# Two transformer blocks on one core: sums of squares in four TensorE strips, splits without GpSimd, the overflow branch in the last expert group

## The chip, the core and the metric

The kernel runs on one core of one Trainium2 chip. The metric is the device time of one execution in microseconds (us); the time of a kernel is the median of its runs. Names: PE is TensorE, DVE is VectorE, ACT is ScalarE, POOL is GpSimd, SP is the queue that issues the loads.

## What is computed

256 tokens of width 1024 go through two blocks. The first has a hybrid mixer (a state-space scan and a gated short convolution, each with a grouped RMS norm) and a mixture of 32 experts; the second has another mixer and a dense feed-forward layer. The change concerns two parts of the first block:

```python
ssd_out = grouped_rmsnorm(y * jax.nn.silu(z), ssd_norm, SSD_GROUPS)   # 2 groups of 512 channels
sc = sc_b * causal_depthwise_conv(sc_c * sc_v, sc_conv_w)
sc_out = grouped_rmsnorm(sc, sc_norm, SC_GROUPS)                      # 16 groups of 64 channels
return jnp.concatenate([ssd_out, sc_out], axis=-1) @ w_out
...
# experts: two of 32 for each token
return (jax.nn.silu(xb @ w_gate[e]) * (xb @ w_up[e])) @ w_down[e]
```

Each expert has a table of a fixed number of tokens. If one gets more, a branch computes the surplus; with these inputs it is not taken.

## The kernel before

**Precision.** Products of the mixer are fp32-exact in three passes: a weight tile of 128x1024 is split into a high and a low half (`hilo`, L316 to 330), the high by ScalarE, the low by `lo_on[0]`, which is VectorE (L330), or GpSimd for the units whose numbers stand in `POOL_A` (42, 43, 45, 47). TensorE then runs high x high, low x high and high x low (L339 to 341 for columns, L309 to 311 for rows).

**The first mixer.** 45 column units (each 128 columns of the input projection: 8 steps of the contraction, 3 products each) and 16 row units of the output projection are run by `run_units`, which splits a unit's weights two units ahead of its products. A table written by hand (`at`, `later`) sets which small steps stand between the units. The last eight column units, 37 to 44, are the gates z: `after_z(j)` multiplies by the row scale (VectorE), takes silu (ScalarE), and multiplies into `xs` (`gate`, L790: GpSimd for j below 6, VectorE for 6 and 7). Units 45 to 60 are the output projection, the short-convolution half first.

**Sums of squares.** For each of the eight 128-channel tiles of the short convolution (`do_scsq`, L875 to 884) and of the scan (`do_ysq`, L770 to 780) ScalarE squares the tile, and one unit later TensorE adds it over the channels with a constant of ones as stationary operand: 16 columns of `half` into rows 0 to 15 of the PSUM tile `sums`, or 2 columns of `col4` into rows 32 and 33. Sixteen fp32 products in all. After the eighth, `rows_rstd` copies the rows out (ScalarE), turns them to tokens by two transposes (L648), computes the reciprocal root on VectorE (L809 and `rsqrt_of`, L242 to 247: a step for the epsilon, two that seed, three rounds of three), and turns them back (L654). `do_sc_scale` and `do_ssd_scale` then scale the tiles, `split_rows` splits them, and the output projection uses them. `route` copies the transposed hidden state, by ScalarE or VectorE, for the router.

**The experts.** Eight groups of four experts: products `g`, then `u`, then down. The four experts of a group run in four strips of 32 rows of the array (`products`, L1184 to 1189; down, L1212). The weights stream through a ring of raw tiles; SP issues each load in program order, when the tile is free, and `products` and `down` issue the loads of a later group behind their own products. The last down tiles are loaded in smaller pieces (`last_loads`).

**The branch.** `overflow()` reads the largest table size on every engine (`values_load`, L1254) and opens a `tc.If`. It stands in the group g = 3 behind the products `u`, before down. At its start and end SP waits until the loads that are out have landed.

Of the kernel before, what the change touches and what calls it, by code (L numbers as in the profile page):

```python
# [8 lines left out]
F32 = mybir.dt.float32  # L9
# [4 lines left out]
ALU = mybir.AluOpType  # L14
# [20 lines left out]
LEAD = 5  # L35
WARM2 = 4
LOP = ()
NRP = ()
SCS = (42, 42, 44, 45)
SPL = (43, 46)  # L40
FS = 2
POOL_A = (42, 43, 45, 47)
W0 = 5
ORDER = (("xs", 2048, 1), ("sc", 2048, 1), ("scc", 1024, 1), ("hnh", 2048, 1), ("hnl", 2048, 1), ("rsb", 256, 1),
         ("bc", 1024, 1), ("wdt", 128, 1), ("dtx", 256, 1), ("ac", 256, 1), ("ach", 256, 1), ("cb", 768, 1),
# [24 lines left out]
def kernel(ctx: ExitStack, tc: tile.TileContext, *aps, dbg=None, stage=9):  # L70
# [120 lines left out]
    alog = const.tile([128, 16], F32, name="alog")  # L191
    nc.gpsimd.dma_start(alog, bass.AP(tensor=A["a_log"].tensor, offset=A["a_log"].offset, ap=[[0, 128], [1, 16]]))

    half = const.tile([128, 30], F32, name="half")
    V.memset(half, 0.0)
    V.memset(half[0:64, 14:15], 1.0)
    V.memset(half[64:128, 15:16], 1.0)
    col4 = const.tile([128, 7], F32, name="col4")
    V.memset(col4, 0.0)
    V.memset(col4[:, 3:4], 1.0)  # L200
    wfirst = const.tile([128, NE], F32, name="wfirst")
# [1 line left out]
    slots = const.tile([128, 128], F32, name="slots")  # L203
    G.iota(slots, pattern=[[1, 128]], base=-FAR, channel_multiplier=0, allow_small_or_imprecise_dtypes=True)
    sel = const.tile([64, 16], F32R, name="sel")
    fold = const.tile([64, 32], F32, name="fold")
    cols1 = const.tile([128, 128], F32, name="cols1")
    cols2 = const.tile([128, 128], F32, name="cols2")
    dskip = const.tile([128, 8], F32, name="dskip")
# [9 lines left out]
    def late_sel():  # L219
        V.memset(sel.bitcast(F32), 0.0)  # L220
        for r in (0, 32):
            V.tensor_copy(sel[r:r + 16, :], ident[:16, :16])
        V.tensor_tensor(fold, ident[0:64, 0:32], ident[0:64, 32:64], op=ALU.add)

    def late_loads():
        ds_ap = A["d_skip"]
# [123 lines left out]
    def later(n, f, *args):  # L350
        at(cur[0] + n, f, *args)
# [14 lines left out]
    def run_units(units, ahead=2, ready=(), pool=lambda i: False):  # L366


        n = len(units)
        ready = list(ready)  # L370
        while len(ready) < min(ahead, n):
            ready.append(units[len(ready)][0]())
        prev = None
        for i in range(n):
            cur[0] = i
            lo_on[0] = G if pool(i + ahead) else V
            for f, args in pre.pop(i, []):
                f(*args)
            if len(ready) <= i + ahead < n:
                ready.append(units[i + ahead][0]())  # L380
            res = units[i][1](ready[i])
            ready[i] = None
            if prev:
                prev()
            for f, args in due.pop(i, []):
                f(*args)
            prev = (lambda f=units[i][2], r=res: f(r)) if units[i][2] else None
        lo_on[0] = V
        cur[0] = n
        if prev:  # L390
            prev()
        while due or pre:
            cur[0] = min([*due, *pre])
            for f, args in pre.pop(cur[0], []) + due.pop(cur[0], []):
                f(*args)
# [183 lines left out]
        across(y, dg)  # L579

    ps = psum_a.enter_context(tc.tile_pool(name="psA", bufs=1, space=PSUM, reuse_waits="tile"))
    sums = ps.tile([64, T], F32, name="sums")

    def scale_rows():
        p = ps.tile([128, T], F32, name="tp", tag="tp")
# [57 lines left out]
    def turned(dst_shape, rows):  # L643

        n = rows.shape[0]
        pt = ps.tile(dst_shape, F32, name="tp", tag="tp")
        for b in range(2):
            P.transpose(pt[:, b, :n], rows[:, b * 128:(b + 1) * 128], ident[:n, :n])  # L648
        return pt
# [117 lines left out]
            P.matmul(p[i * 64:(i + 1) * 64, 128:256], xdt["t"][:, 1, c], e[:, i, 256:384], start=False, stop=True)  # L767
        V.scalar_tensor_tensor(xs[:, j, :], xs[:, j, :], dskip[:, j:j + 1], p, op0=ALU.mult, op1=ALU.add)

    def do_ysq(j):  # L770
        sq = work.tile([128, T], F32, name="sq", tag="sq", bufs=2)
        S.activation(sq, xs[:, j, :], AF.Square)
        g = j // 4

        def sm():
            P.matmul(sums[32:34, :], col4[:, 3 - g:5 - g], sq, start=(j == 0), stop=(j == 7))
            if j == 7:
                rows_rstd(sums[32:34, :], 2, 512, "ssd")

        later(1, sm)  # L780


    def after_z(j):
        def f(o):
            z = work.tile([128, T], F32, name="cacc", tag="cacc", bufs=2)
            V.tensor_tensor(z, o, rsb, op=ALU.mult)
            S.activation(z, z, AF.Silu)

            def gate():
                (G if j < 6 else V).tensor_tensor(xs[:, j, :], xs[:, j, :], z, op=ALU.mult)  # L790
                later(1, do_ysq, j)

            later(j < 7, gate)
            if j % 4 == 3:
                load_next()

        return f
# [2 lines left out]

    def rows_rstd(src, n, c, key):

        v = work.tile([16, T], F32, name="rr", tag="rr")
        sst[key] = hl = work.tile([64, T], F32R, name="hl", tag="hl")
        V.memset(hl.bitcast(F32), 0.0)
        S.activation(v[:n], src, AF.Copy, scale=1.0 / c)

        def mid():
            V.tensor_scalar(ts32[0][:, :, :n], turned([128, 2, 16], v[:n])[:, :, :n], EPS, None, op0=ALU.add)  # L809
            x, y, t = [i[:, :, :n] for i in ts32]  # L810
            (rsqrt_pool if key in NRP else rsqrt_of)(x, y, t)

        def end():
            stacked(hl, turned_back(ts32[1], n)[:n], n)

        later(1, mid)
        later(2, end)
# [55 lines left out]
        return f  # L873

    def do_scsq(j):  # L875
        sq = work.tile([128, T], F32, name="sq", tag="sq", bufs=2)
        S.activation(sq, sc[:, j, :], AF.Square)

        def sm():
            P.matmul(sums[0:16, :], half[:, 14 - 2 * j:30 - 2 * j], sq, start=(j == 0), stop=(j == 7))  # L880
            if j == 7:
                rows_rstd(sums[0:16, :], 16, 64, "sc")

        later(1, sm)

    def src(nm):
        return lambda: R[nm]
# [63 lines left out]
    def route(a, n=None):  # L951

        if not ROUTED:
            ROUTED["h"] = work.tile([128, 8, T], F32, name="hT", tag="xdt")
        hT = ROUTED["h"]
        if n is None:
            L = ROUTED[a] = ps.tile([128, 36], F32, name="L", tag="acb", bufs=2)
            for k in range(8):
                P.matmul(L, hT[:, k, a * 128:(a + 1) * 128], wr[:, k, :], start=(k == 0), stop=(k == 7))
            return  # L960
        pt = ps.tile([128, 4, 128], F32, name="tp", tag=("mm", "tp", "mm", "yp")[2 * a + n], bufs=(3, 1, 3, 1)[2 * a + n])
        for kk in range(4):
            P.transpose(pt[:, kk, :], h[:, a, n * 512 + kk * 128:n * 512 + (kk + 1) * 128], ident)
        d = hT[:, 4 * n:4 * n + 4, a * 128:(a + 1) * 128]
        if n:
            V.tensor_copy(d, pt)
        else:
            S.activation(d, pt, AF.Copy)
# [16 lines left out]
    korder = list(range(8, 16)) + list(range(8))  # L985
    units += [row_unit(k, i) for i, k in enumerate(korder)]
    at(48, lambda: S.activation(small.tile([128, 1], F32, name="one"), ones[:, 0:1], AF.Sqrt))
    run_units(units, ready=early, pool=lambda i: i in POOL_A)

    ss = small.tile([128, 2], F32, name="ss")  # L990
    L = [ROUTED[a] for a in range(2)]
# [136 lines left out]
    with ExitStack() as pp:  # L1128
# [51 lines left out]
        def products(g, m):  # L1180

            p = P1[m] = ps.tile([128, 512], F32, name="p1", tag="p1", bufs=2)
            for k in range(8):
                for i in range(4):  # L1184
                    r = slice(32 * i, 32 * i + 32)
                    P.matmul(p[r], XS[g][:, k, r], ew(4 * g + i, m, k), start=(k == 0), stop=(k == 7))  # L1186
            for i in range(4):
                if (4 * g + i, m) not in odd:
                    load_expert()
# [15 lines left out]
        def down(g, fs):  # L1205
            if g not in PY:
                PY[g] = [ps.tile([128, 512], F32, name=f"py{n}") for n in range(2)]
            for f in fs:
                for n in range(2):
                    for i in range(4):  # L1210
                        r = slice(32 * i, 32 * i + 32)
                        P.matmul(PY[g][n][r], HT4[g][:, f, r], ew(4 * g + i, "d", f)[:, n * 512:(n + 1) * 512],  # L1212
                                 start=(f == 0), stop=(f == 3))
            if 3 in fs:
                for i in range(4):
                    if (4 * g + i, "d") not in odd:
                        load_expert()

        ysb = {}

# [173 lines left out]
        for g in range(NG):  # L1394
            end = g == NG - 1
            products(g, "g")
            gate_silu()
            if g == 0:
                gates()
                slots_of(1)  # L1400
            else:
                for a, n, _ in HALF:
                    combine(g - 1, a, n)
            slots_back(g)
            slots_turn(g)
            if end:
                for i in range(4):
                    h_turned(i)
            products(g, "u")
            turn(g)  # L1410
            if not end:
                gather(g + 1, 0)
                gather(g + 1, 1)
            if g < NG - 2:
                slots_of(g + 2)
            if g == 1:
                block2_consts()
            if g == 3:
                overflow()
            if end:  # L1420
                mr_stack.close()
                pools2()
                down(g, range(3))
                keep_warm(ps, WARM3, "p2")
                down(g, [3])
                split2(1)
            else:
                down(g, range(4))
            y_out(g)
# [612 lines left out]
```

## Time and profile before

| | |
|---|---|
| median of three runs | 1019.81 us (1016.51 to 1022.83) |
| profiled execution, its own time | 1019.49 us |
| its span | 1017.7 us |
| TensorE busy | 878.6 us (86%) |
| VectorE busy | 433.2 us (43%) |
| ScalarE busy | 318.9 us (31%) |
| GpSimd busy | 146.6 us (14%) |
| read from HBM | 285.87 MB, 282 GB/s over the span |

The span is cut into three stages: the first mixer, the experts, the second block. The shares are means over stages that have different limits, so a share is read within one stage. The durations in the rows below come from this one execution.

### The profile page before, as it was taken

Reading aid. Unit: us, or ns where it says so; the run is one execution under the profiler, and the core shown is the slowest. Engines: PE = TensorE matmul, PEld = TensorE weight load, DVE = VectorE, ACT = ScalarE, POOL = GpSimd, SP = SyncE. Lnnn points to the kernel's source line nnn. Section 1 sums busy time; section 2 is a strip of 40 time slices with the busy share of each in tenths; the row PEclk is TensorE's granted clock in tenths of the full one; section 3 lists DMA queues with packets and bytes.
Section 4 is the critical chain, followed back from the end, with each engine's and each line's share of the span. In section 5 each row is a group of like instructions: output and inputs, shape, how many; then the busy total and the mean of one; then the engine's idle time right before and its main releaser. Section 6 shows DMA issues by size and latency. Waiting matters only on the chain.

```text
span 1017.7 us, 13571 instructions
## 1 busy us (share of the span) xinstructions
PE 878.6 (86%) x5631; PEld 622.3 (61%) x5632; DVE 433.2 (43%) x756; ACT 318.9 (31%) x533; POOL 146.6 (14%) x126
## 2 busy tenths in 40 slices
PE   9989998999978677696667869689689999999997
PEld 8988887678424224241322415137568789999996
DVE  6897575564110111101001110017896776555554
ACT  5565454534001101000000100006355555444444
POOL 4323024002000000000000000003432232111112
PEclk9999999999998789787778988799889999999999
DMA  9496324268999999998999999999625345575301
GB/s 295 114 389 222 138 112 153 95 225 336 425 428 429 427 426 430 426 425 352 427 428 427 428 428 428 428 410 379 232 83 207 96 153 166 169 245 170 120 1 42
DMA packets 77824, 287.85 MB, mean 283 GB/s; under 512 B 12547, under 2 KB 41406, under 8 KB 66238
## 3 DMA queue, kind: packets, MB, share of 16 engines
q1 hardware_dynamic: 77062, 285.55, 71.6%
q8 instruction: 46, 0.75, 0.3%
q0 software_dynamic: 448, 1.08, 0.3%
q10 hardware_dynamic: 248, 0.30, 0.1%
q14 instruction: 20, 0.16, 0.0%
HBM read 285.87 MB, written 1.05 MB: 282 GB/s over the span
## 4 chain that ended last, share of the span: by engine, by line
PE 33%; DMA 13%; DVE 5%; ACT 1%; issue 1%; POOL 0%; SPq 0%; DVEq 0%; ACTq 0%; POOLq 0%
DMA raw<-in_w_up_dram 11%; PE mm L339 5%; PE mm L341 5%; PE mm L340 5%; PE po L309 3%; PE po L311 3%; PE po L310 3%; PE p L1186 3%; PE py L1212 3%; PE gp L1169 2%; DMA rawx<-in_w_down_dram 2%; DVE xf L1528 1%; DVE wab L1493 0%; PE op L1676 0%; PE op L1678 0%
## 5 line engine op out<-in xcount | busy, mean ns | idle before, releaser
L1186 PE MATMUL p<-raw,xse 128*32 128x512 f32 x1008 | 182.5, 722 | 82.6 <-DMA raw<-in_w_gate_dram 48.3
L339 PE MATMUL mm<-hnh,hi 128*128 128x256 f32 x808 | 232.7, 288 | 2.0 <-ACT cx L702 1.3
L341 PE MATMUL mm<-hnh,lo 128*128 128x256 f32 x808 | 227.9, 282 | 1.5 <-DVE lo L330 1.4
L340 PE MATMUL mm<-hnl,hi 128*128 128x256 f32 x808 | 227.3, 281 | 0.0
L330 DVE TENSOR_TENSOR lo<-raw,hi 128x1024 fp32r<-128x1024 f32 x137 | 168.9, 1237 | 80.5 <-ACT hi L329 80.5
L329 ACT ACTIVATE hi<-raw 128x1024 fp32r<-128x1024 f32 x152 | 159.1, 1057 | 100.7 <-PE mm L340 39.8
L1186 PEld LDWEIGHTS p<-raw,xse 128*32 128x32 f32 x1008 | 40.3, 129 | 214.7 <-issue 94.0
L339 PEld LDWEIGHTS mm<-hnh,hi 128*128 128x128 f32 x808 | 152.8, 189 | 11.4 <-issue 7.5
L341 PEld LDWEIGHTS mm<-hnh,lo 128*128 128x128 f32 x808 | 152.8, 189 | 2.5 <-DVE lo L330 2.3
L340 PEld LDWEIGHTS mm<-hnl,hi 128*128 128x128 f32 x808 | 153.2, 190 | 0.9
L1249 DVE TENSOR_TENSOR h<-h,pc 128x512 f32<-128x512 f32 x32 | 20.5, 684 | 140.2 <-PE pc L1247 140.2
L1374 POOL TENSOR_TENSOR g<-h,gain 128x512 f32<-128x512 f32 x2 | 3.5, 1786 | 461.8 <-DVE h L1249 461.8
L1169 PE MATMUL gp<-oh,xnf 128*128 128x128 f32 x256 | 64.6, 412 | 5.1 <-ACT xse L1176 5.1
L1169 PEld LDWEIGHTS gp<-oh,xnf 128*128 128x128 f32 x256 | 62.1, 334 | 6.4 <-ACT xse L1176 6.4
L1212 PE MATMUL py<-raw,hs 128*32 128x512 f32 x480 | 64.5, 635 | 1.2 <-ACT hs L1203 0.7
L1198 DVE TENSOR_TENSOR sg<-sg,p 128x512 f32<-128x512 f32 x8 | 5.5, 688 | 113.4 <-PE p L1186 113.4
L1193 ACT ACTIVATE sg<-p 128x512 f32<-128x512 f32 x8 | 4.8, 599 | 148.3 <-PE p L1186 138.0
L1927 POOL TENSOR_TENSOR sgf<-sgf,rsb 128x256 f32<-128x256 f32 x22 | 31.7, 1441 | 134.4 <-ACT sgf L1926 134.4
L1203 ACT ACTIVATE hs<-p 128x512 f32<-128x512 f32 x8 | 4.8, 597 | 135.7 <-PE p L1201 135.7
L330 POOL TENSOR_TENSOR lo<-raw,hi 128x1024 fp32r<-128x1024 f32 x15 | 37.3, 2499 | 39.7 <-ACT hi L329 39.7
L1212 PEld LDWEIGHTS py<-raw,hs 128*32 128x32 f32 x480 | 19.9, 116 | 32.4 <-issue 27.7
L1174 DVE COPY xse<-gp 128x512 f32<-128x512 f32 x8 | 5.5, 692 | 74.8 <-PE gp L1169 74.8
(469 smaller groups left out, 1160.6 us busy)
## 6 DMA issues: line engine op xcount, KB each, us to landing
raw<-in_w_gate_dram SPq DMA_DIRECT2D x32, 2048.0 KB
raw<-in_w_up_dram SPq DMA_DIRECT2D x31, 2048.0 KB
raw<-in_w_down_dram SPq DMA_DIRECT2D x27, 2048.0 KB
raw<-in_w_in_dram SPq DMA_DIRECT2D x14, 2048.0 KB
raw<-in_w_ffn_in_dram SPq DMA_DIRECT2D x22, 1024.0 KB
raw<-in_w_out_dram SPq DMA_DIRECT2D x6, 2048.0 KB
raw<-in_w_ffn_out_dram SPq DMA_DIRECT2D x5, 2048.0 KB
raw<-in_w_down_dram SPq DMA_DIRECT2D x12, 512.0 KB
```

The costliest lines, as they stand in the source:

```text
L309: P.matmul(po[a, j], yh[:, ts], wh[:, 0, ns], start=(i == 0), stop=False)
L310: P.matmul(po[a, j], yh[:, ts], wl[:, 0, ns], start=False, stop=False)
L311: P.matmul(po[a, j], yl[:, ts], wh[:, 0, ns], start=False, stop=end)
L329: S.activation(hv[:, r], src[:, r], AF.Copy)
L330: lo_on[0].tensor_tensor(lv, src, hv.bitcast(F32), op=ALU.subtract)
L339: P.matmul(o, wh, xh, start=first, stop=False)
L340: P.matmul(o, wh, xl, start=False, stop=False)
L341: P.matmul(o, wl, xh, start=False, stop=last)
L1169: P.matmul(p[:, kk, :], xn[:, a, 4 * hf + kk::8], OT[g][:, a, :], start=(a == 0), stop=(a == 1))
L1186: P.matmul(p[r], XS[g][:, k, r], ew(4 * g + i, m, k), start=(k == 0), stop=(k == 7))
L1212: P.matmul(PY[g][n][r], HT4[g][:, f, r], ew(4 * g + i, "d", f)[:, n * 512:(n + 1) * 512], start=(f == 0), stop=(f == 3))
L1927: G.tensor_tensor(t, t, rsb, op=ALU.mult)
```

## The change

1. **Sums.** `do_scsq` and `do_ysq` call a new `quarter_sums`. Squares are kept until there are four; one unit after the fourth, four products of 32 columns each write four strips of 32 rows of a `sums` tile [128, 2, 256]. The second four add to the same strips. `rows_rstd` copies 128 rows, and two products with a constant `fold` add the four strips and turn them to tokens, in place of the two transposes. `half`, `col4` and `fold` get wider. The squares lie in four buffers, two of them taken from `dtx` and `ac`.
2. **GpSimd.** `POOL_A` goes, so the low halves of units 42, 43, 45 and 47 are made by VectorE; the gate products of j below 6 move to VectorE too. An option for a reciprocal root on GpSimd, unused before, is removed.
3. **Router copy.** One of four copies of the transposed state (second half of the columns, second half of the tokens) moves from VectorE to ScalarE.
4. **Branch.** `overflow()` moves from group 3 to the last group, behind its products `g`, the combine step and the slots, ahead of `h_turned` and of the products `u`. The loads that `products(7, "g")` issued are now issued behind the branch (`next_loads`).

```diff
-POOL_A = (42, 43, 45, 47)
...
-        V.tensor_tensor(fold, ident[0:64, 0:32], ident[0:64, 32:64], op=ALU.add)
+        V.tensor_tensor(fold, ident[:, 0:16], ident[:, 32:48], op=ALU.add)
+        for i in (64, 96):
+            V.tensor_tensor(fold, fold, ident[:, i:i + 16], op=ALU.add)
...
-    sums = ps.tile([64, T], F32, name="sums")
+    sums = ps.tile([128, 2, T], F32, name="sums")
...
+    def quarter_sums(m, j, x, sel_, key, n, c):
+        q = j % 4
+        if q == 0:
+            sqs[m] = []
+        four = sqs[m]
+        sq = work.tile([128, T], F32, name="sq", tag=("sq", "sq", "dtx", "ac")[q], bufs=2 if q < 2 else 1)
+        S.activation(sq, x, AF.Square)
+        four.append(sq)
+        def sm():
+            for i in range(4):
+                P.matmul(sums[32 * i:32 * i + 32, m, :], sel_(j - 3 + i), four[i], start=(j == 3), stop=(j == 7))
+            if j == 7:
+                rows_rstd(sums[:, m, :], n, c, key)
+        if q == 3:
+            later(1, sm)
...
     def do_ysq(j):
-        sq = work.tile([128, T], F32, name="sq", tag="sq", bufs=2)
-        S.activation(sq, xs[:, j, :], AF.Square)
-        g = j // 4
-        def sm():
-            P.matmul(sums[32:34, :], col4[:, 3 - g:5 - g], sq, start=(j == 0), stop=(j == 7))
-            if j == 7:
-                rows_rstd(sums[32:34, :], 2, 512, "ssd")
-        later(1, sm)
+        quarter_sums(1, j, xs[:, j, :], lambda j: col4[:, 3 - j // 4:35 - j // 4], "ssd", 2, 512)
...
-                (G if j < 6 else V).tensor_tensor(xs[:, j, :], xs[:, j, :], z, op=ALU.mult)
+                V.tensor_tensor(xs[:, j, :], xs[:, j, :], z, op=ALU.mult)
...
-        v = work.tile([16, T], F32, name="rr", tag="rr")
+        v = work.tile([128, T], F32, name="rr", tag="rr")
-        S.activation(v[:n], src, AF.Copy, scale=1.0 / c)
+        S.activation(v, src, AF.Copy, scale=1.0 / c)
         def mid():
-            V.tensor_scalar(ts32[0][:, :, :n], turned([128, 2, 16], v[:n])[:, :, :n], EPS, None, op0=ALU.add)
+            pt = ps.tile([128, 2, 16], F32, name="tp", tag="tp")
+            for b in range(2):
+                P.matmul(pt[:, b, :n], v[:, b * 128:(b + 1) * 128], fold[:, :n], start=True, stop=True)
+            V.tensor_scalar(ts32[0][:, :, :n], pt[:, :, :n], EPS, None, op0=ALU.add)
...
-        if n:
+        if n > a:
             V.tensor_copy(d, pt)
...
-    run_units(units, ready=early, pool=lambda i: i in POOL_A)
+    run_units(units, ready=early)
...
+            if (g, m) != (NG - 1, "g"):
+                next_loads(g, m)
+        def next_loads(g, m):
             for i in range(4):
                 if (4 * g + i, m) not in odd:
                     load_expert()
...
             if end:
+                overflow()
+                next_loads(g, "g")
                 for i in range(4):
                     h_turned(i)
             products(g, "u")
...
-            if g == 3:
-                overflow()
```

TensorE, between the last column unit and the first row unit, before (`sums` is the sum of squares, `po` the output projection, `scb` the row scale of the short convolution):

```order
L341 MATMUL mm<-hnh,lo 128x256
L835 MATMUL scb<-hl,selb 128x256 x2
L776 MATMUL sums<-sq,col_131 2x256
L309 MATMUL po<-hi,yhi 128x512
L310 MATMUL po<-lo,yhi 128x512
L311 MATMUL po<-hi,ylo 128x512
```

and of the change:

```order
L341 MATMUL mm<-hnh,lo 128x256
L852 MATMUL scb<-hl,selb 128x256 x2
L783 MATMUL sums<-sq,col_131 32x256 x4
L309 MATMUL po<-hi,yhi 128x512
L310 MATMUL po<-lo,yhi 128x512
L311 MATMUL po<-hi,ylo 128x512
```

One sum has become four products into strips; the sums that stood in other units are gone.

VectorE, around the reciprocal root of the short convolution (from `ts<-tp`), before (`lo` is a low half, `cacc` a product of z by the row scale):

```order
L330 TENSOR_TENSOR lo<-raw,hi 128x1024
L786 TENSOR_TENSOR cacc<-mm,rsb 128x256
L805 MEMSET hl 64x256
L786 TENSOR_TENSOR cacc<-mm,rsb 128x256
L809 TENSOR_SCALAR ts_288<-tp 128x32
L242 TENSOR_SCALAR ts_290<-ts_288 128x32
```

and of the change:

```order
L330 TENSOR_TENSOR lo<-raw,hi 128x1024
L799 TENSOR_TENSOR cacc<-mm,rsb 128x256
L803 TENSOR_TENSOR xs<-xs,cacc 128x256
L819 MEMSET hl 64x256
L330 TENSOR_TENSOR lo<-raw,hi 128x1024
L799 TENSOR_TENSOR cacc<-mm,rsb 128x256
L803 TENSOR_TENSOR xs<-xs,cacc 128x256
L826 TENSOR_SCALAR ts_288<-tp 128x32
L242 TENSOR_SCALAR ts_290<-ts_288 128x32
```

A split and two gate products that GpSimd made now stand ahead of the chain in VectorE's queue.

SP, where the branch ends, before:

```order
L1322 REGISTER_ALU
L1322 COMPARE_AND_BRANCH
L1322 UNCONDITIONAL_BRANCH
L1254 UNCONDITIONAL_BRANCH
L443 DMA raw<-in_w_up_dram 128x4096 x4
L443 DMA raw<-in_w_down_dram 128x4096 x4
L443 DMA raw<-in_w_gate_dram 128x4096 x4
```

and of the change:

```order
L1333 REGISTER_ALU
L1333 COMPARE_AND_BRANCH
L1333 UNCONDITIONAL_BRANCH
L1265 UNCONDITIONAL_BRANCH
L457 DMA raw<-in_w_down_dram 128x1024 x3
L432 DMA rawx<-in_w_down_dram 128x1024
L457 DMA raw<-in_w_down_dram 128x1024 x3
L432 DMA rawx<-in_w_down_dram 128x1024
```

Behind the branch now stand the pieces of the last down tiles, where whole tiles of the next groups stood.

## Rows read from the trace of the kernel before

**Rows 1.** The page: busy tenths of TensorE and GB/s, 40 slices.
```profile
PE   9989998999978677696667869689689999999997
...
GB/s 295 114 389 222 138 112 153 95 225 336 425 428 429 427 426 430 426 425 352 427 428 427 428 428 428 428 410 379 232 83 207 96 153 166 169 245 170 120 1 42
```

**Rows 2.** Timeline of TensorE: start, us, engine, line, operation, out<-in, shapes, count, [idle before].
```profile
146.68 0.28 PE L340 MATMUL mm<-hnl,hi 128*128 128x256 f32 x1
146.80 0.28 PE L341 MATMUL mm<-hnh,lo 128*128 128x256 f32 x1
...
147.76 0.28 PE L340 MATMUL mm<-hnl,hi 128*128 128x256 f32 x1
...
174.54 0.59 PE L776 MATMUL sums<-sq,col 128*2 128x256 f32 x2
175.07 0.39 PE L339 MATMUL mm<-hnh,hi 128*128 128x256 f32 x1
```

**Rows 3.** Timeline of TensorE at its longest idle stretch in the mixer.
```profile
165.31 0.28 PE L341 MATMUL mm<-hnh,lo 128*128 128x256 f32 x1
168.57 0.59 PE L654 MATMUL tp<-ident,ts 128*16 128x128 f32 x2 [2.97 <-DVE ts L247]
...
170.41 0.41 PE L340 MATMUL mm<-hnl,hi 128*128 128x256 f32 x1
```

**Rows 4.** Windows: sum, PE, PEld, DVE, ACT, POOL (xcount), granted clock, DMA share, GB/s.
```profile
160.00:170.00 10.00, 7.03 (x50) 5.42 (x48) 6.23 (x14) 3.37 (x8) 6.83 (x5) 0.92 0.03 12
170.00:180.00 10.00, 10.00 (x68) 8.70 (x68) 5.71 (x10) 5.12 (x8) 3.80 (x4) 0.91 0.58 210
180.00:190.00 10.00, 10.00 (x49) 6.79 (x48) 5.65 (x11) 4.72 (x8) 2.41 (x1) 1.00 0.08 15
```

**Rows 5.** Timeline of VectorE: the chain of the reciprocal root.
```profile
162.56 0.19 DVE L809 TENSOR_SCALAR ts<-tp 128x32 f32<-128x32 f32 x1 [3.33 <-PE tp L648]
...
163.85 2.30 DVE L245 SCALAR_TENSOR_TENSOR ts<-ts 128x32 f32<-128x32 f32 x1
...
168.00 0.19 DVE L246 TENSOR_TENSOR ts<-ts,ts 128x32 f32<-128x32 f32 x1
168.23 0.19 DVE L247 SCALAR_TENSOR_TENSOR ts<-ts,ts 128x32 f32<-128x32 f32 x1
```

**Rows 6.** Timeline of GpSimd in the same stretch.
```profile
160.67 2.41 POOL L330 TENSOR_TENSOR lo<-raw,hi 128x1024 fp32r<-128x1024 f32 x1 [5.91 <-ACT hi L329]
```

**Rows 7.** Timeline of SP's issues, around group 3 and in the last group.
```profile
438.60 2.86 SPq L443 DMA_DIRECT2D raw<-in_w_gate_dram  x4
469.92 1.88 SPq L443 DMA_DIRECT2D raw<-in_w_up_dram  x4
...
638.62 1.75 SPq L443 DMA_DIRECT2D raw<-in_w_up_dram  x4
659.80 1.28 SPq L457 DMA_DIRECT2D raw<-in_w_down_dram  x3
```

**Rows 8.** Waits of SP: line, what it waited for, us in all, times, longest.
```profile
SPq L1254 <- SPq L1254: 27.2, 6, 5.3
```

**Rows 9.** Windows behind the branch, columns as in rows 4.
```profile
465.00:470.00 5.00, 2.06 (x6) 0.22 (x9) 0.00 (x0) 0.00 (x0) 0.00 (x0) 0.50 0.46 197
470.00:475.00 5.00, 5.00 (x28) 1.18 (x24) 0.00 (x0) 0.00 (x0) 0.00 (x0) 0.50 0.85 272
```

**Rows 10.** The chain that ended last: start, us, engine, name, line, count; down products.
```profile
511.96 8.04 PE py L1212 x64
```

**Rows 11.** The page, costliest groups: the low halves on VectorE; mean ns behind busy us.
```profile
L330 DVE TENSOR_TENSOR lo<-raw,hi 128x1024 fp32r<-128x1024 f32 x137 | 168.9, 1237 | 80.5 <-ACT hi L329 80.5
```

**Rows 12.** Instructions of L790 on VectorE: ns least/median/most, first and last start.
```profile
L790 DVE TENSOR_TENSOR xs<-xs,cacc x2: 418/418/418, 187.0 to 187.3; 128x256 f32<-128x256 f32 x2
```

**Rows 13.** The chain that ended last, at the last group.
```profile
670.28 10.18 DMA rawx<-in_w_down_dram
...
690.79 1.90 PE py L1212 x10
```

More of the change, by code (lines that the diff above doesn't have):

```diff
@@ L37 @@
 LOP = ()
-NRP = ()
 SCS = (42, 42, 44, 45)
@@ L192 @@
     nc.gpsimd.dma_start(alog, bass.AP(tensor=A["a_log"].tensor, offset=A["a_log"].offset, ap=[[0, 128], [1, 16]]))
-    half = const.tile([128, 30], F32, name="half")
+    half = const.tile([128, 46], F32, name="half")
     V.memset(half, 0.0)
@@ L197 @@
     V.memset(half[64:128, 15:16], 1.0)
-    col4 = const.tile([128, 7], F32, name="col4")
+    col4 = const.tile([128, 35], F32, name="col4")
     V.memset(col4, 0.0)
@@ L205 @@
     sel = const.tile([64, 16], F32R, name="sel")
-    fold = const.tile([64, 32], F32, name="fold")
+    fold = const.tile([128, 16], F32, name="fold")
     cols1 = const.tile([128, 128], F32, name="cols1")
@@ L768, in do_y @@
         V.scalar_tensor_tensor(xs[:, j, :], xs[:, j, :], dskip[:, j:j + 1], p, op0=ALU.mult, op1=ALU.add)
-    def do_ysq(j):
-        sq = work.tile([128, T], F32, name="sq", tag="sq", bufs=2)
-        S.activation(sq, xs[:, j, :], AF.Square)
-        g = j // 4
-        def sm():
-            P.matmul(sums[32:34, :], col4[:, 3 - g:5 - g], sq, start=(j == 0), stop=(j == 7))
-            if j == 7:
-                rows_rstd(sums[32:34, :], 2, 512, "ssd")
-        later(1, sm)
+    def quarter_sums(m, j, x, sel_, key, n, c):
[13 more added lines that the diff above has]
+            later(1, sm)
+    sqs = {}
+    def do_ysq(j):
+        quarter_sums(1, j, xs[:, j, :], lambda j: col4[:, 3 - j // 4:35 - j // 4], "ssd", 2, 512)
     def after_z(j):
@@ L801, in rows_rstd @@
     def rows_rstd(src, n, c, key):
-        v = work.tile([16, T], F32, name="rr", tag="rr")
+        v = work.tile([128, T], F32, name="rr", tag="rr")
         sst[key] = hl = work.tile([64, T], F32R, name="hl", tag="hl")
         V.memset(hl.bitcast(F32), 0.0)
-        S.activation(v[:n], src, AF.Copy, scale=1.0 / c)
+        S.activation(v, src, AF.Copy, scale=1.0 / c)
         def mid():
-            V.tensor_scalar(ts32[0][:, :, :n], turned([128, 2, 16], v[:n])[:, :, :n], EPS, None, op0=ALU.add)
+            pt = ps.tile([128, 2, 16], F32, name="tp", tag="tp")
+            for b in range(2):
+                P.matmul(pt[:, b, :n], v[:, b * 128:(b + 1) * 128], fold[:, :n], start=True, stop=True)
+            V.tensor_scalar(ts32[0][:, :, :n], pt[:, :, :n], EPS, None, op0=ALU.add)
             x, y, t = [i[:, :, :n] for i in ts32]
-            (rsqrt_pool if key in NRP else rsqrt_of)(x, y, t)
+            rsqrt_of(x, y, t)
         def end():
@@ L875, in do_scsq @@
     def do_scsq(j):
[L876 to L884, printed above, removed]
+        quarter_sums(0, j, sc[:, j, :], lambda j: half[:, 14 - 2 * j:46 - 2 * j], "sc", 16, 64)
     def src(nm):
@@ L1214, in down @@
             if 3 in fs:
-                for i in range(4):
-                    if (4 * g + i, "d") not in odd:
-                        load_expert()
+                next_loads(g, "d")
         ysb = {}
```

## Prediction

> **What bounds the kernel now.** I read the busy slices first [rows 1]. The reader is to see three stages. In the first nine slices of 25.4 us (the first mixer ends in the tenth, at about 240 us) TensorE (PE) stands at 8 or 9 and the loads at 95 to 389 GB/s: TensorE is the bound, and time taken from its queue there moves everything behind it. In slices 11 to 26 (the experts, whose last loads land in the 27th) the loads run at 425 to 430 GB/s but for one slice at 352, and TensorE mostly at 6 to 9: the weight stream is the bound. It starts when the mixer's last splits free the ring buffers, so it moves with the mixer's end. From 690 us the second block follows, in which the change edits nothing.
>
> Three places touch the change. First, a sum of squares costs TensorE more than its own time [rows 2]. Two products of the mixer start 0.12 us apart (146.68 and 146.80). Between 146.80 and 147.76 stand one sum and one further product, 0.96 us where two spacings would be 0.24: a sum alone costs 0.72 us. Behind another narrow or fp32 product the switch is already paid, and it costs 0.53 us (174.54 to 175.07).
>
> Second, the one large idle stretch of TensorE in the mixer [rows 3]: the last product starts at 165.31, the transposes that bring back the reciprocal roots of the second half start at 168.57, after 2.97 us of idleness that VectorE's (DVE's) last step L247 ended. When it resumes it is slow: a product takes 0.41 us (170.41) where it took 0.28 (147.76), the lower of its two clock levels (1.2 against 2.4 GHz), and the granted clock of the two ten-microsecond windows is 0.92 and 0.91 [rows 4].
>
> Why VectorE is late [rows 5]: the chain has 12 small steps. At its end they start 0.23 us apart (168.00, 168.23); the fourth, of the same size, took 2.30 us. GpSimd (POOL) was at a split of 2.41 us when the chain began [rows 6], and the kernel has a gate product and a second split follow there.
>
> Third, the overflow branch. The queue SP issues four loads at 438.60 and the next at 469.92 [rows 7]; between them it stood in six waits of the branch's line, 27.2 us together [rows 8], until the four had landed. Behind that wait the stream ran dry: 197 and 272 GB/s in two windows of 5 us [rows 9].
>
> **The change part by part.** *Sums.* Sixteen products become four groups of four, which write four 32-partition strips. Four groups stay at the places where the fourth and eighth sum stood, so twelve go: four alone (4 x 0.72 = 2.9), seven behind other narrow work (7 x 0.53 = 3.7), and one of a pair (0.4): 7.0 us. What a group costs above one sum is bounded by two rows. If the four run one behind the other, each of the 12 further ones adds its own time. That is 0.43 us: the 0.53 less one switch of 0.1, as 0.72 less 0.53 is 0.19 for the two switches of a sum alone. It takes 5.2 us, and 1.8 us of gain are left. If they run side by side as the experts' products do, the addition is small: 64 passes of 512 columns in strips of 32 took 8.04 us [rows 10], 0.50 us for four, so 0.25 us for four of 256 columns, and as a sum is fp32 and makes two passes, 0.50 us against 0.43 for one. The groups have the experts' form, so I take the lower bound and 0.1 us for each group: 6.6 us of gain. The two products with the constant that folds the strips stand where two transposes stood and produce the same 16 or 2 columns: nothing.
>
> The Trainium skill speaks against this part: its page TensorEngine Tiling (Array Packing), Key Properties, says that changing the tiling mode drains TensorE. The mixer's products use the whole array and the groups would enter and leave the strips four times, but rows 2 show that a sum into 16 or 2 columns pays 0.1 us at each end already. By the rule with a further spacing at each end the gain would be some 0.8 us less; the sum here stays at 6.6.
>
> *No splits and gates on GpSimd.* Four splits move to VectorE at 1.24 us [rows 11] and six gate products at 0.42 us [rows 12]: 7.4 us more there. With GpSimd silent, the chain should take 12 x 0.23 = 2.8 us: from 162.56 to about 165.4. TensorE comes for it when the product of 165.31 has ended, at 165.6. So the idle 2.97 us goes. With it goes the slow stretch: a mean clock of 0.92 and 0.91 over two windows is 0.8 + 0.9 = 1.7 us of full-speed time; some of it may lie in the idleness, so I take 1.4. Together 4.4 us; if the chain starts late, as little as 0.
>
> What hides the 7.4 us: VectorE is busy 17.6 of the 30 us from 160 to 190 [rows 4], some 3.1 us of that because the chain is stretched (162.56 to 168.42 is 5.9, less 2.8). About 22 us of work for 23 us of TensorE's shortened time is near the limit, with splits two units ahead of TensorE as the cover. In the new order [the DVE rows of the change] a split and a gate stand ahead of the chain and a further split ahead of the row halves. I charge 0.3 us for small waits. What would be late next is the low half of the first four scaled short-convolution tiles, or the fourth square, at the first product of the output projection; if this cover fails the whole 4.4 us is lost.
>
> *One hT copy from VectorE to ScalarE (ACT)* at the mixer's end, one instruction of one size on either engine: nothing. The wider constants, made once before the mixer: nothing.
>
> *The branch.* Group 3 gets back what rows 9 miss: at 428 GB/s [rows 1] ten microseconds carry 4280 kB, the windows show 5 x (197 + 272) = 2345, so 1935 kB or 4.5 us. In the last group SP meets the same wait. It issues the last full-size loads (638.62), then stands until they have landed, and only then issues the last down slices, which before went out from 659.80 while the stream was full [rows 7]. The chain shows those loads landing at 670.28 and the last slice being used at 690.79 [rows 13]: 20.5 us of stream behind the wait that nothing else covers. So 4.5 us is given back at one place and paid at the other: net 0. Bounds: 4.5 us gained if the second wait costs nothing, 3 lost if the slices restart worse and TensorE, waiting, runs the turn to block two at the lower clock. I take 0, as both waits have the same form: four loads out, then none until they land. The branch's own steps on TensorE stand ahead of transposes that wait for the last up tile anyway.
>
> *Sum.* 6.6 + 4.4 - 0.3 + 0 = 10.7 us. The profiled run took 1019.49 us (span 1017.7 and 1.8 around it), close to the median 1019.81. Forecast: 1019.5 - 10.7 = 1008.8 us. The mixer's gain reaches the end because the stream that bounds the experts starts with the mixer's end.
>
> **The rivals.** *Strips do not overlap.* The four run in turn, or each group drains TensorE: 1.8 instead of 6.6, 1013.6 us. For it: four groups stand alone among full-array products; against: rows 10. Chance 0.07.
>
> *VectorE takes the stall over.* Idleness at the chain, or the same amount at the projection's start, stays: 4.4 less, 1013.2 us. For it: 22 us of work in 23. Against: two units of lead. 0.16.
>
> *The branch dearer at the end*: 3 us, 1011.8 us, 0.09. *The branch free at the end*, the restart covered by the small slices: 4.5 more, 1004.3 us, 0.10. Against both: the same wait, with the stream as the bound on either side.
>
> *VectorE paces the z units (slower).* In one queue stand split, z product, row halves; in ScalarE's stand silu, square, the next split's high part. If each waits for the other in a ring, a unit takes the sum: 1.24 for the low half and as much, an estimate, for the high one, 0.42 each for product, silu and square by their size [rows 11, 12], and 0.9 as a share of the two products that scale by rows, about 4.6 us. TensorE needs 24 products at the spacing of 0.12 [rows 2], 2.9 us, and a sum, so 3.3. Over nine units the difference of 1.3 us is 12 us, and with two more slow-clock stretches of 1.4 it is 14.8, and of the gains only that of the sums is left: 1019.5 + 14.8 - 6.6 = 1027.7 us. It decides from the point at which the two-unit lead (6.6 us) is used up in the first half of the stretch. Against it: ScalarE is busy only 13.2 of 30 us [rows 4]. 0.07.
>
> **How the numbers follow.** Forecast 0.51, with its own range 1006 to 1011.5. The range of 1003.5 to 1016 takes in the free branch, the strips, the dearer branch and the lost stall, and leaves out the slower case and the tails. A measurement here tells about 1% from no change, 10.2 us, so the forecast lies at that edge. Faster by over 1%: two thirds of the forecast's cases, the free branch and a part of the others, 0.47. Slower by over 1%: 0.05 of the slower case and 0.02 for what is not thought of, 0.07. Within 1%: 0.46.
>
> **What would show it.** Strips right: four groups of some 0.6 us in TensorE's queue and a mixer shorter by 6 to 7 us before the stall counts. Chain right: 12 steps of 0.2 us each with no step over 0.4, no wait of TensorE over 0.5 us between 150 and 200 us, a granted clock of 1.00 there. Branch right: no slice under 420 GB/s around 460 us, and a hole of the same 4 to 5 us at about 655 to 662 us. The forecast is wrong if the projection's first product waits for a low half or a square, if a group takes over 1.5 us, or if the hole at the end is missing or much wider.

## The result and the profile after

The changed kernel takes 1008.43 us (median of four runs, 1007.45 to 1011.62) against 1019.87 for the kernel before beside it: a ratio of 0.9899, interval 0.9875 to 0.9922, which is 8.0 to 12.7 us less. The forecast was 1008.8. The profiled execution has a span of 1006.6 us, 11.1 less than before.

The page's slices, PE and GB/s as in [rows 1]:

```profile
PE   8999999999869676776967687788689999999997
...
GB/s 297 112 388 233 151 102 167 168 222 412 428 428 425 427 430 426 426 428 426 428 428 426 428 428 427 387 360 380 180 90 204 120 132 168 189 230 183 111 1 42
```

The reader is to see that the slice of 352 is gone, that the tenth slice is at 412 instead of 336, so the stream starts earlier, and that slices 26 and 27 are at 387 and 360: the hole has moved.

Timeline of TensorE in the changed kernel, a group of four strips between two column products (answers to [rows 2]) and the transposes at the end of the reciprocal root ([rows 3]):

```profile
154.37 0.28 PE L341 MATMUL mm<-hnh,lo 128*128 128x256 f32 x1
154.58 0.64 PE L783 MATMUL sums<-sq,half 128*32 128x256 f32 x8
155.15 0.38 PE L339 MATMUL mm<-hnh,hi 128*128 128x256 f32 x1
155.37 0.28 PE L340 MATMUL mm<-hnl,hi 128*128 128x256 f32 x1
...
161.47 0.38 PE L654 MATMUL tp<-ident,ts 128*16 128x128 f32 x2
```

From 154.37 to 155.37 is 1.00 us, less two spacings of 0.12: a whole group costs 0.76 us, where one sum alone cost 0.72. And no idleness stands before the transposes at 161.47, where it was 2.97.

Timeline of VectorE, the first and the last steps of the chain ([rows 5]):

```profile
158.68 0.19 DVE L826 TENSOR_SCALAR ts<-tp 128x32 f32<-128x32 f32 x1
...
159.33 0.19 DVE L245 SCALAR_TENSOR_TENSOR ts<-ts 128x32 f32<-128x32 f32 x1
...
160.91 0.19 DVE L246 TENSOR_TENSOR ts<-ts,ts 128x32 f32<-128x32 f32 x1
161.13 0.19 DVE L247 SCALAR_TENSOR_TENSOR ts<-ts,ts 128x32 f32<-128x32 f32 x1
```

Twelve steps in 2.6 us, the fourth as short as the rest. The windows of the same stretch ([rows 4]):

```profile
160.00:170.00 10.00, 10.00 (x83) 9.67 (x82) 8.38 (x19) 3.76 (x9) 0.00 (x0) 1.00 0.32 97
170.00:180.00 10.00, 10.00 (x55) 7.55 (x53) 7.69 (x14) 6.41 (x11) 0.00 (x0) 1.00 0.27 116
180.00:190.00 10.00, 10.00 (x52) 7.54 (x51) 8.08 (x19) 7.06 (x12) 0.00 (x0) 1.00 0.60 211
```

In these 30 us TensorE is busy throughout at full clock; VectorE is busy for 24.2 of them, and TensorE does not wait for it.

SP's issues at group 3 and in the last group ([rows 7]):

```profile
425.66 1.75 SPq L443 DMA_DIRECT2D raw<-in_w_gate_dram  x4
444.74 1.75 SPq L443 DMA_DIRECT2D raw<-in_w_up_dram  x4
...
622.46 1.75 SPq L443 DMA_DIRECT2D raw<-in_w_up_dram  x4
654.66 2.38 SPq L457 DMA_DIRECT2D raw<-in_w_down_dram  x3
```

the waits of the branch's line ([rows 8]):

```profile
SPq L1265 <- SPq L1265: 29.2, 7, 4.9
```

and the windows of the new hole ([rows 9]):

```profile
650.00:655.00 5.00, 4.63 (x27) 4.66 (x28) 0.00 (x0) 0.00 (x0) 0.00 (x0) 0.66 0.40 169
655.00:660.00 5.00, 5.00 (x47) 1.89 (x50) 0.00 (x0) 0.00 (x0) 0.00 (x0) 1.00 0.82 281
```

Two rows of the changed kernel answer to nothing in the kernel before: TensorE waits for the routing table at the mixer's end, 0.19 and 0.86 us, 1.05 together.

```profile
229.86 0.19 PE L1079 MATMUL pr<-At,strict 128*128 128x32 bf16 x1 [0.19 <-DVE At L1103]
230.91 0.18 PE L1080 MATMUL pr<-At,strict 128*128 128x32 bf16 x1 [0.86 <-DVE At L1103]
```

**Where the time went, read from the stream.** The experts' stage is bound by bytes, so I asked when a given sum of bytes had landed. The GB/s of windows of 2 us, times 2 us, were added up from the span's start. First row: us at which the sum reaches so many MB, in the kernel before; below, the difference to it in one profiled execution of each kernel. The other kernels are those of the next section.

| MB | 60 | 140 | 160 | 220 | 230 | 250 |
|---|---|---|---|---|---|---|
| before | 271.2 | 458.5 | 509.7 | 650.2 | 674.0 | 731.0 |
| changed kernel | -11.8 | -11.9 | -16.2 | -16.2 | -11.5 | -10.3 |
| sums alone (first execution) | -8.7 | -8.5 | -8.5 | -8.5 | -8.5 | -8.3 |
| sums alone (second execution) | -7.8 | -7.7 | -7.6 | -7.5 | -7.5 | -7.3 |
| splits and gates | -2.1 | -2.2 | -1.7 | -1.7 | -1.8 | -1.5 |
| splits alone | -4.6 | -4.6 | -4.1 | -4.1 | -4.2 | -4.2 |
| gates alone | -1.4 | -1.3 | -0.8 | -0.8 | -0.8 | -0.9 |
| branch alone | 0.2 | 0.1 | -4.4 | -4.4 | 2.6 | 2.8 |
| changed, branch back | -12.0 | -11.9 | -11.6 | -11.5 | -11.5 | -11.3 |
| changed, one strip | -6.6 | -6.5 | -10.9 | -10.9 | -5.8 | -5.4 |
| changed, no branch | -13.0 | -13.1 | -17.5 | -17.5 | -17.5 | -17.0 |
| changed, copy back | -11.6 | -11.5 | -16.0 | -15.9 | -8.5 | -8.1 |
| changed, copy back, loads first | -12.2 | -12.2 | -16.6 | -16.6 | -16.5 | -14.9 |
| changed, loads first | -10.2 | -10.3 | -14.7 | -14.7 | -14.6 | -12.1 |

The changed kernel comes out of the mixer 11.8 us early, gains 4.3 at group 3 (between 140 and 160 MB), and gives 4.7 back at the last group (220 to 230). Every kernel whose branch has left group 3 gains 4.3 to 4.5 us there. Every kernel whose branch stands ahead of the last loads gives 4.7 to 7.4 us back at the last group. The row of splits and gates and the last row lag behind their neighbours from 60 MB on; in these two executions TensorE's clock had fallen shortly before, as told at the end.

### The profile page after: what moved, and what is told of

Read it like the earlier page. It is cut to its first block, busy times and chain, and to the rows that moved or that the text cites. A ratio compares the mean times of both kernels' runs of the same rounds, so it can differ in the third digit from the quotient of the medians.

```text
span 1006.6 us, 13584 instructions
## 1 busy us (share of the span) xinstructions
PE 869.4 (86%) x5635; PEld 620.3 (62%) x5636; DVE 435.5 (43%) x767; ACT 318.8 (32%) x534; POOL 133.3 (13%) x116
## 3 DMA queue, kind: packets, MB, share of 16 engines
HBM read 285.87 MB, written 1.05 MB: 285 GB/s over the span
## 5 line engine op out<-in xcount | busy, mean ns | idle before, releaser
L330 DVE TENSOR_TENSOR lo<-raw,hi 128x1024 fp32r<-128x1024 f32 x141 | 173.8, 1237 | 79.0 <-ACT hi L329 78.4
L311 PE MATMUL po<-hi,al 128*128 128x512 f32 x88 | 34.8, 396 | 0.0
```

Source lines behind the costliest of these rows:

```text
L311: P.matmul(po[a, j], yl[:, ts], wh[:, 0, ns], start=False, stop=end)
L330: lo_on[0].tensor_tensor(lv, src, hv.bitcast(F32), op=ALU.subtract)
```

## The experiments

Ratios are against the kernel before, run beside each.

**Sums alone**: the kernel before with `quarter_sums`, `rows_rstd` and the constants of the change.

> Kernel before with the sums by four strips alone; the splits and gates on GpSimd and the branch stay. My theory (the strips run side by side): 12 products fewer, 6.6 us off, 1013.2 us; TensorE's idle stretch at the reciprocal root stays near 3 us. Rival, strips in turn: 1.8 us off, 1018.0 us. Rival, the saved time is swallowed by a longer idle stretch: under 4 us off.

1010.64 us, ratio 0.9915 (0.9896 to 0.9934): 8.7 us off by the ratio (6.7 to 10.6), more than the 6.6 of the sum. The idle stretch stayed, 3.02 us. A part of what went besides is in the windows: the granted clock is 1.00 behind the idle stretch, where [rows 4] has 0.92 and 0.91.

```profile
160.00:170.00 10.00, 6.99 (x56) 6.51 (x55) 8.10 (x18) 3.33 (x7) 3.73 (x3) 1.00 0.16 28
170.00:180.00 10.00, 10.00 (x67) 8.21 (x66) 6.44 (x11) 6.15 (x11) 7.99 (x4) 1.00 0.43 184
```

**The same kernel, a second execution.**

> The kernel with the sums by strips alone once more, for a second look at TensorE's clock behind the idle stretch of 3.0 us. If the order with grouped sums keeps the clock up, the windows from 160 to 180 us show 1.00 again; if a drop behind such an idle stretch comes and goes between executions, they can show less than 1.00 this time. The time: 1010 to 1013 us.

1011.45 us in one run, and TensorE's clock has dropped behind the stretch:

```profile
160.00:170.00 10.00, 6.99 (x44) 6.43 (x44) 6.70 (x15) 3.61 (x7) 3.37 (x4) 0.83 0.16 36
170.00:180.00 10.00, 10.00 (x72) 8.36 (x71) 5.74 (x11) 5.96 (x10) 6.59 (x4) 1.00 0.41 175
```

So behind the same idle stretch the clock falls in one execution and not in another. The sums have not removed the drop.

**One strip.**

```diff
-                P.matmul(sums[32 * i:32 * i + 32, m, :], sel_(j - 3 + i), four[i], start=(j == 3), stop=(j == 7))
+                P.matmul(sums[0:32, m, :], sel_(j - 3 + i), four[i], start=(j == 3 and i == 0), stop=(j == 7 and i == 3))
...
-        S.activation(v, src, AF.Copy, scale=1.0 / c)
+        S.activation(v[:32], src[:32], AF.Copy, scale=1.0 / c)
...
-                P.matmul(pt[:, b, :n], v[:, b * 128:(b + 1) * 128], fold[:, :n], start=True, stop=True)
+                P.matmul(pt[:, b, :n], v[:32, b * 128:(b + 1) * 128], fold[:32, :n], start=True, stop=True)
```

> Changed kernel with the four products of each group into one and the same strip of 32 rows, one behind the other; the number of groups and all that follows stay. My theory (the gain comes from the strips working side by side): each group is longer by 3 x 0.43 us, four groups 5.2 us, 1013.6 us. Rival (the gain comes from fewer switches, grouping alone is enough): within 1.5 us of the changed kernel, 1009.9 us or less.

1014.05 us, ratio 0.9951 (0.9934 to 0.9968). TensorE's timeline:

```profile
155.43 0.28 PE L341 MATMUL mm<-hnh,lo 128*128 128x256 f32 x1
155.64 1.91 PE L783 MATMUL sums<-sq,half 128*32 128x256 f32 x8
157.48 0.39 PE L339 MATMUL mm<-hnh,hi 128*128 128x256 f32 x1
157.70 0.29 PE L340 MATMUL mm<-hnl,hi 128*128 128x256 f32 x1
```

2.27 us less 0.24 is 2.03 for the group, 1.27 above the group in four strips: 0.42 for each further product. Four groups make 5.1 us, and the time rose by 5.6. The gain comes from the strips working side by side; grouping alone is worth 1.7 of the 6.8 us.

**No GpSimd, and its two halves.** Three kernels from the one before: both, `POOL_A = ()` alone, and the gate products alone.

```diff
-POOL_A = (42, 43, 45, 47)
+POOL_A = ()
...
-                (G if j < 6 else V).tensor_tensor(xs[:, j, :], xs[:, j, :], z, op=ALU.mult)
+                V.tensor_tensor(xs[:, j, :], xs[:, j, :], z, op=ALU.mult)
```

> Kernel before with the four splits and six gate products on VectorE alone; the sums and the branch stay. My theory: the idle 2.97 us and the slow clock behind it go, 4.4 us off less 0.3 of small waits, 1015.7 us, and the twelve steps of the chain start 0.23 us apart. Rival, VectorE takes the stall over: 1019 to 1020 us, with waits of TensorE for VectorE between 150 and 200 us.

> Kernel before with the four splits moved to VectorE and the gate products left on GpSimd. Theory: the split of 2.41 us on GpSimd stretches VectorE's chain; without it the idle stretch at the chain is under 1 us, 3.5 us or more off, 1016.3 us. Rival (the gate products stretch it as well): half of the idle stretch stays, 1018 us.

> Kernel before with the six gate products moved to VectorE and the four splits left on GpSimd. Theory after the run with the splits alone (idle stretch 0.3 us): the split of 2.41 us on GpSimd is what stretches VectorE's chain, so the idle stretch stays at 2 us or more and the time within 1 us of before, 1018.5 to 1020 us. Rival (either half of GpSimd's work is enough to stretch it, or the gates count as much): idle stretch under 1 us, 3 us or more off.

Both: 1014.61 us, ratio 0.9948 (0.9930 to 0.9965), no wait of TensorE from 100 to 250 us, clock 1.00 from 100 to 230 us. From 230 to 240 us it is 0.66, with no wait ahead of it; this profiled execution took 1018.05 us, the longest of its six runs, so the median is the better measure here. Splits: 1015.25 us, 0.9959 (0.9944 to 0.9973), 0.29 us idle. Gates: 1017.9 us, 0.9990 (0.9977 to 1.0002), 2.0 us idle. The splits are most of it. Why shows best in the first run with the sums alone, where GpSimd's work is still there. Its timeline:

```profile
156.89 2.39 POOL L332 TENSOR_TENSOR lo<-raw,hi 128x1024 fp32r<-128x1024 f32 x1 [4.76 <-ACT hi L331]
159.24 0.73 POOL L805 TENSOR_TENSOR xs<-xs,cacc 128x256 f32<-128x256 f32 x1
159.93 2.38 POOL L332 TENSOR_TENSOR lo<-raw,hi 128x1024 fp32r<-128x1024 f32 x1
162.27 0.72 POOL L805 TENSOR_TENSOR xs<-xs,cacc 128x256 f32<-128x256 f32 x1
```

and VectorE's:

```profile
158.82 0.19 DVE L828 TENSOR_SCALAR ts<-tp 128x32 f32<-128x32 f32 x1 [3.49 <-PE tp L827]
159.04 0.28 DVE L244 TENSOR_SCALAR ts<-ts 128x32 int32<-128x32 int32 x1
159.35 0.66 DVE L245 TENSOR_SCALAR ts<-ts 128x32 int32<-128x32 int32 x1
160.04 2.32 DVE L247 SCALAR_TENSOR_TENSOR ts<-ts 128x32 f32<-128x32 f32 x1
162.40 0.65 DVE L248 TENSOR_TENSOR ts<-ts,ts 128x32 f32<-128x32 f32 x1
163.08 0.19 DVE L249 SCALAR_TENSOR_TENSOR ts<-ts,ts 128x32 f32<-128x32 f32 x1
```

Each of the last three GpSimd instructions holds one step of VectorE for about its own length: 0.66 beside 0.73, 2.32 beside 2.38, 0.65 beside 0.72. Under the split before them, which ends at 159.28, the step that reads `tp` from PSUM (158.82) took its usual 0.19 us; only the next one, which reads SBUF, stood until the split was over. With the gates moved, one step of 2.31 us is left, beside the second split.

**The branch alone, and the branch back.** The first moves `overflow()` and `next_loads` in the kernel before as the change does; the second undoes that in the changed kernel:

```diff
             if end:
-                overflow()
                 next_loads(g, "g")
...
+            if g == 3:
+                overflow()
```

> Kernel before with the branch moved to the last group alone. My theory: a hole in the stream is moved, 0 to 0.5 us slower, 1019.8 to 1020.3 us. Rival, the hole at the end is hidden: 4.5 us off, 1015.3 us. Rival, dearer at the end: 3 us more, 1022.8 us.

> Changed kernel with the branch put back into group 3, the loads of the last group in their old order of issue. Theory (the hole is moved, and at the end it is as dear or a little dearer): 0 to 1.5 us faster than the changed kernel, 1007 to 1008.4 us. Rival (the move is a gain): 2 us or more slower, 1010.5 us.

1020.56 us, ratio 1.0005 (0.9991 to 1.0019), and 1007.58 us, ratio 0.9888 (0.9869 to 0.9907): the move is worth nothing, or costs some 0.8 us. With the branch back SP stands at group 3 again:

```profile
426.36 2.28 SPq L443 DMA_DIRECT2D raw<-in_w_gate_dram  x4
458.35 1.88 SPq L443 DMA_DIRECT2D raw<-in_w_up_dram  x4
```

By the table the branch costs 4.3 to 4.5 us at group 3 and at the end 4.7 (changed kernel), 5.1 (one strip), 7.0 (branch alone) and 7.4 (copy back). Why the restart behind the same branch differs so much between these four executions is open.

**No branch.** `overflow()` is left out, and with it the surplus of a table.

> Changed kernel without the branch; the surplus of an expert's table is left out of the computation. Theory: the hole of some 5.5 us in the weight stream of the last group goes, and all of it reaches the end: 1003 us. Rival (the hole is partly hidden by the tail of the last group): 2 us or less off, 1006.4 us or more.

1001.93 us, ratio 0.9831 (0.9814 to 0.9849): 6.5 us under the changed kernel. The hole reaches the end in full: by the table the two are 6.0 us apart at 230 MB, 1.2 of them from the mixer already (60 MB), so 4.8 for the hole.

**The router copy.** The wait at 230 us made me doubt my "nothing".

```diff
-        if n > a:
+        if n:
```

> Changed kernel with the one router copy back on VectorE. New theory, from the trace of the changed kernel: on ScalarE the copy delays the two squares behind it by about 0.5 us, VectorE's reciprocal waits for them 1.34 us, and TensorE waits 1.05 us for the routing table at 230 us; with the copy back TensorE does not wait there and about 1.0 us goes, 1007.4 us. Rival, as predicted: nothing, 1008.4 us.

1009.49 us, ratio 0.9901 (0.9881 to 0.9920): no gain. The wait at 230 us went, as the theory said, and yet the time did not: that theory has fallen. The table shows why. By 60 MB the stream is 11.6 us ahead without the wait and 11.8 with it, though with it TensorE reaches the gather of the first experts only 10.8 us early (231.97 against 242.81): the stream is already running and does not see the wait. The end time alone would not have told, because this execution paid 7.4 us at the branch where that of the changed kernel paid 4.7.

**Loads ahead of the branch.** SP drains whatever it has issued, so the last slices can be in flight during the wait. Two scratch tiles of the branch are shared to leave buffers for them; the copy is back on VectorE.

```diff
-                overflow()
                 next_loads(g, "g")
+                overflow()
...
-                y = split.tile([128, D], F32, name="oy", tag="hi", bufs=4)
+                y = xt.rearrange("p a b -> p (a b)")
...
-                wts = [split.tile([128, 2, 512], F32, name=f"owt{i}", tag="lo", bufs=4) for i in range(2)]
+                wts = [split.tile([128, 2, 512], F32, name=f"owt{i}", tag="lo", bufs=4) for i in range(1)] * 2
```

> Changed kernel with the router copy back on VectorE and the last down slices issued ahead of the branch (two scratch tiles of the branch are shared to make room). Theory: the last group's stream has no hole and the last slice comes 5 us earlier; the hole falls on the first loads of the second block, which are needed by its first split, so 2 to 3 us of it come back: 1004 to 1005 us. Rival (the second block waits for all of it): 1007.4 us, as with the copy back alone.

> The changed kernel with the last down slices issued ahead of the branch, and the router copy where the change put it, on ScalarE: one line from the kernel with both edits (1003.9 us). If the copy is worth nothing, because the stream is full while TensorE waits for the routing table: 1003.2 to 1004.6 us. If its wait of 1.05 us reaches the end: 1005 us.

1003.92 us, ratio 0.9846 (0.9829 to 0.9863), with the copy on VectorE, and 1004.38, 0.9848 (0.9829 to 0.9866), with it on ScalarE: better than both kernels. Between the two the copy makes no difference that is clear of the noise; an effect of 1 us would not show at these intervals. SP now meets the wait behind the last slice:

```profile
665.72 0.33 SPq L432 DMA_DIRECT2D rawx<-in_w_down_dram  x1
676.21 1.02 SPq L489 DMA_DIRECT2D raw<-in_w_in_dram  x2
```

and the hole falls on the second block's first loads:

```profile
670.00:675.00 5.00, 4.78 (x31) 2.39 (x32) 0.00 (x0) 0.00 (x0) 0.00 (x0) 1.00 0.52 206
675.00:680.00 5.00, 4.81 (x35) 2.61 (x30) 1.84 (x4) 2.11 (x5) 0.00 (x0) 1.00 0.49 157
```

There TensorE is busy for 9.6 of 10 us: it is the bound, and the stream can afford the hole. Of the 4.8 us of the hole 2.0 are left against the kernel without a branch.

## Why the prediction was right

**Sums, 6.6 us.** Right, by its own steps. A group costs 0.04 us above a sum alone, not 0.1, so the term is 6.8. The second execution of the sums alone, which has the slow clock where the kernel before has it, is 7.8 us ahead at 60 MB; where the other 1.0 us comes from is not traced here. The rule of the Trainium skill (TensorEngine Tiling (Array Packing), Key Properties) that a change of the tiling mode drains TensorE showed no price beyond what a single sum pays already: 0.76 us with strips among full-array products against 0.72 without. The rival that they don't overlap is excluded by the one-strip run.

**The chain, 4.4 us less 0.3.** Right: 4.2 us with the splits alone and 5.3 with both (intervals 2.8 to 5.7 and 3.6 to 7.1). Its cause was named and is now shown in rows. The Trainium skill states it too: the page SBUF — State Buffer, Who interferes with whom, says that GpSimd and some instructions of VectorE share a pair of ports, and that whoever issues first has it for the whole instruction; 2.32 beside 2.38 us agrees. The part of it that I put on the clock, 1.4, is a mean over executions that differ: [rows 4] lose 1.7, and an execution may lose nothing. By medians the parts, run alone, add up to more than the whole: 9.2 for the sums, 5.3 for GpSimd and -0.7 for the branch make 13.8, and the change brought 11.4 (by the ratios 13.5 and 10.3). Each of these four numbers has an interval of 1.4 to 2.4 us to either side, so by the times alone the excess is not clear of the noise. In the traces the drop explains it. At 60 MB the splits alone are 4.6 us ahead. The sums' second execution, with the drop as in the kernel before, is 7.8 ahead, which makes 12.4 against 11.8 for the whole change. Their first execution, without that drop by chance, is 8.7 ahead and makes 13.3: the drop is then counted twice, as the runs without GpSimd's splits lose it by their making.

**VectorE as the next bound.** Not reached, but near: 24.2 of 30 us busy. The rival that it takes the stall over, and the slower case, where it paces the units, find no wait of TensorE for it from 100 to 220 us.

**The router copy, nothing.** The number was right, the reason was not: the copy does delay TensorE by 1.05 us at the mixer's end, and what hides it is the stream, which I had not named.

**The branch, net 0.** Right: 4.3 gained and 4.7 paid in the profiled execution, and the run of it alone is at 1.0005. That this execution paid 4.7 is in part luck: two of the four executions with the same wait paid 7.0 and 7.4, close to the rival that is 3 us dearer. I expected the drain at either place and found it; what I did not see is that one of the two orders of loads and branch is free of most of it.

## What to carry to other kernels

A wait that empties the load queue cost this saturated stream 4.3 us or more at either place; put it where the stream is not the bound, and issue what is needed before it. Four narrow products that write different strips of 32 rows went side by side for about the price of one (0.76 against 0.72 us). And look at GpSimd before moving work to it: the small steps that TensorE waits for, where they read SBUF, stood still on VectorE for as long as one of GpSimd's instructions ran.

## What was not expected of the hardware

TensorE's clock behind an idle stretch of some 3 us at the same place in the program: two executions of the sums-alone kernel show 1.00 and 1.00, and 0.83 and 1.00, in the windows 160 to 170 and 170 to 180 us; the kernel before shows 0.92 and 0.91, and the branch-alone kernel 0.84 and 0.82. By full-speed time that is 0, 1.7, 1.7 and 3.4 us, in code that is the same up to there but for the sums. The clock also fell where no wait stood ahead. With splits and gates moved it is 0.66 from 230 to 240 us, and in the kernel with the loads first and the copy on ScalarE 0.75 and 0.91 from 220 to 240. TensorE is busy all through both stretches; around the fall it ran two groups of sixteen products of 36 columns for the router, and the other executions ran the same ones at full clock. Either drop is 3.4 us of full-speed time, and at 60 MB these two streams are 2.5 and 2.0 us behind their neighbours in the table (splits alone; copy back, loads first). From 50 to 60 us six executions, among them the changed kernel and both of the sums alone, show 0.83 where the kernel before shows 1.00; TensorE waits between 60 and 80 us in the kernel before (busy for 9.72 and 9.28 of 10 us) and less in the changed one (10.00 and 9.64), so a part of that loss is taken up by waits.

The drops may be a part of the spread of the kernel before, 1016.51 to 1022.83 us; that is not shown, since only profiled executions show the clock.
